# A higher scheduling priority for the chain of states of each head pair in an RWKV-7 layer

## The chip, the cores and the metric

The kernel runs on one core of one Trainium2 chip. The metric is the device time of one execution in microseconds (us). The engines are named as in the profile: PE (TensorE, with PEld for its weight loads), DVE (VectorE), ACT (ScalarE), POOL (GpSimd) and SP (SyncE, which issues most transfers here). Each engine works through its own list of instructions in order; semaphores tie the lists together.

## What is computed

A backbone of two layers over 256 latent tokens of width 1024 with 256 context tokens in front. Layer 0 is a bidirectional RWKV-7 mixer followed by a grouped top-2 mixture of experts, layer 1 a short gated convolution and again experts. The change lies in the mixer's recurrence. Each of 16 heads has a 64x64 state, updated once per token, in both directions; the context is scanned first, and its final state starts the scan over the latent tokens:

```python
def _wkv_scan(decay, k, v, kk, a, r, s0, reverse):
    def step(s, inp):
        w_t, k_t, v_t, kk_t, a_t, r_t = inp
        sa = jnp.einsum('bhvk,bhk->bhv', s, -kk_t)
        s = (s * w_t[:, :, None, :] + sa[..., None] * (kk_t * a_t)[:, :, None, :]
             + v_t[..., None] * k_t[:, :, None, :])
        y = jnp.einsum('bhvk,bhk->bhv', s, r_t) if with_output else None
        return s, y
    return lax.scan(step, s0, xs, reverse=reverse)
...
for p, reverse in enumerate((False, True)):
    s_ctx, yc = _wkv_scan(dec_c, kd_c, v_c, kk_c, a_c, None, s0, reverse)
    _, yl = _wkv_scan(dec_l, kd_l, v_l, kk_l, a_l, r_l, s_ctx, reverse)
    y_lat.append(yl + _bonus(r_l, kd_l, v_l, r_k))
```

The two directions are added, normed per head, multiplied by a gate and projected with w_o. The experts and the second layer follow.

## The kernel before

The recurrence is done in chunks of 64 tokens: 8 chunks (NCH), 4 of context (group g = 0) and 4 of latent tokens (g = 1). Two heads share the 128 partitions, so there are 8 pairs, `fb` = 0 to 7. For each pair the work falls into parts, each written as a Python generator that yields between small pieces:

- **first, second, pre** (together `both`): decays, keys and the operators of all chunks for both directions. The scan `ls` (L704, L706), `kd`, `at`, `bk` (L727 to L744) on DVE; products `pab`, `pat`, `pq` on PE (L766 to L792); `apl`, `at_bd`, `gq`, `hk` copied out of PSUM by ACT (L768, L779, L786, L794); masked into `b_bd`, `gq`, `hk` by DVE (L774, L799, L796).
- **inverse**: the triangular systems of all chunks of the pair at once. ACT packs `apl` into `a_d` (L808, four copies), DVE transposes it (L813), does 31 steps of two operations, a product `lv` (L820) and a subtraction from `t_l` (L822), each reading the result before it, and transposes back into `t_d` (L824). `a_l`, `t_l`, `t_d` exist once, so the inverses of two pairs follow each other.
- **solve**: ACT spreads `t_d` into `d_bd` (L831, four copies for each direction); products (L843) and evictions (`kd`, `bk`, L853 to L862) put the inverse into the operators `rd` and `hk` (L869, L872).
- **chain**: 8 chunk steps for each of two directions, in turn. A step multiplies into a PSUM tile `po` (two buffers): `hk` by the values (L886), plus `rd` by the state `s_bd` of the step before (L893). DVE copies one head's new state out of `po` (L896), ACT the other's (L897), 14 copies each in a pair. In the latent chunks the output goes to `yt`, copied by ACT (L901) for the first direction to reach a chunk and added by DVE (L903) for the second.
- **finish**: bonus, group norm and gate of `yt` (L914 to L938).

What overlaps is written in the loop over pairs. While pair `cur` is solved, half of the next pair's inverse, the finish of the pair before and modulation columns (`adas`) are emitted beside it; while `cur`'s chain runs, the rest of that inverse and the operators of the pair after next (`both(nn)`):

```python
drive((seq(solve(cur, 0), solve(cur, 1)), 20), (half, SPLIT), (finish(prev) if prev else None, 3), ...)
if nxt:
    load_late(nxt)
    drive((chain(cur), 16), (inv, 33 - SPLIT), (both(nn) if nn else None, 22), (adas(ADA2[fb]), ADA2[fb]))
```

`drive` takes turns among its generators in proportion to the weights. That gives the order in which instructions are emitted, and with it their priority. The order on the engines is not this one: a list scheduler goes over the whole program, and of the instructions that its own model holds ready it gives each engine the one of highest priority. So an instruction emitted late can still be placed early when nothing ahead of it is ready. The last pair's chain runs after the loop, under `urgent(..., 200)`, beside the projection `project`.

Of the kernel before, what the change touches and what calls it, by code (L numbers as in the profile page):

```python
# [30 lines left out]
SPLIT = 22  # L31
# [98 lines left out]
class Kern:  # L130
# [63 lines left out]
    def adas(self, n):  # L194
        for _ in range(n):
            if self.todo:
                for _ in self.ada(*self.todo.pop(0)):
                    pass
                yield
# [395 lines left out]
    def rwkv_wkv(self, project_v, right, h, outer):  # L595

        tc, nc, io = self.tc, self.nc, self.io
        with ExitStack() as es:
# [54 lines left out]
            def load(fb):  # L653
                q = Pair()
                q.fb = fb
                q.fs = fs = slice(fb * P, fb * P + P)
                q.kt = two.tile([P, TT], F32, tag="kt", name="kt", bufs=1)
                nc.sync.dma_start(q.kt, self.k_d[fb])
                q.kk = two.tile([P, TT], F32, tag="kkh", name="kkh", bufs=1)
                nc.sync.dma_start(q.kk, self.kk_d[fb])  # L660
                l2 = two.tile([P, 4 * P], F32, tag="l2", name="l2", bufs=1)
                nc.sync.dma_start(l2, io["lora2"][fb][:, :4 * P])
                q.l2 = [two.tile([P, 4 * P], F32R, tag=f"l2{i}", name=f"l2{i}", bufs=1) for i in range(2)]
                nc.scalar.copy(q.l2[0], l2)
                (nc.vector if fb in L2E else nc.gpsimd).tensor_sub(q.l2[1], l2, q.l2[0].bitcast(F32))
                q.rt = two.tile([P, T], F32, tag="rt", name="rt", bufs=1)
                nc.sync.dma_start(q.rt, self.r_d[fb])
                q.ea = [None] * 2
                q.yg = h[:, fb, :]
                q.b = [b_bd[2 * (fb % 2) + d] for d in range(2)]  # L670
                q.at = [at_bd[2 * (fb % 2) + d] for d in range(2)]
                q.rd, q.hk, q.gq = maps[fb % 3]["rd"], maps[fb % 3]["hk"], maps[fb % 2]["gq"]
                return q

            def load_late(q):
                fb, fs = q.fb, q.fs
                q.vt = two2.tile([P, 2, P], F32, tag="vt", name="vt", bufs=2)
                nc.sync.dma_start(q.vt, self.v_d[TC:TT, fs].rearrange("(a p) f -> p a f", p=P))
                q.g2 = two2.tile([P, P], F32, tag="g2", name="g2", bufs=2)
                nc.sync.dma_start(q.g2, io["lora2"][fb][:, 4 * P:])  # L680
                q.vbd = v_bd[fb % 2]
                halves(lambda h, hs: nc.sync.dma_start(
                    q.vbd[hs, :, hs], self.v_d[:, fb * P + 64 * h:fb * P + 64 * h + 64]
                    .rearrange("(c s) f -> s c f", s=64)))
# [117 lines left out]
            def inverse(q):  # L802


                for b in range(4):
                    qs = slice(32 * b, 32 * b + 32)
                    cs = slice(32 * (b % 2), 32 * (b % 2) + 32)
                    nc.scalar.copy(a_d[qs], q.apl.rearrange("p d c t -> p (d c) t")[qs, :, cs])  # L808
                nc.gpsimd.memset(t_l, 0.0)
                for a in range(2):  # L810
                    pcopy(t_l.rearrange("p m r -> p (m r)")[:, a:a + 511:34],
                          self.k("unit", a, a + 1).broadcast_to([P, 16]))
                nc.vector.transpose(out=a_l.rearrange("p j (a u) -> p j a u", a=2),  # L813
                                    in_=a_d.rearrange("p u j -> p j u").unsqueeze(2).broadcast_to([P, 32, 2, 16]))
                yield
                for kk in range(31):
                    m, n = kk // 2 + 1, 31 - kk
                    u = el.tile([P, 144], F32, tag="lv", name="lv")
                    u = u[:, :m * n].rearrange("p (c i) -> p c i", i=n)
                    nc.vector.tensor_mul(u, a_l[:, kk:kk + 1, kk + 1:].broadcast_to([P, m, n]),  # L820
                                         t_l[:, 0:m, kk:kk + 1].broadcast_to([P, m, n]))
                    nc.vector.tensor_sub(t_l[:, 0:m, kk + 1:], t_l[:, 0:m, kk + 1:], u)  # L822
                    yield
                nc.vector.transpose(out=t_d.rearrange("p u j -> p j u"), in_=t_l)  # L824
                yield
# [49 lines left out]
            def chain(q):  # L875
                q.yt = yt = two2.tile([P, 2, P], F32, tag="yt", name="yt", bufs=1)
                po = [[None] * NCH for _ in range(2)]

                def where(i, d):
                    return i // 4, (3 - i % 4 if d else i % 4)  # L880

                def hpart(i, d):
                    g, j = where(i, d)
                    m = 64 if g == 0 else P
                    po[d][i] = pc.tile([P, 512], F32, tag="pc", name="po")[:m, :P]
                    nc.tensor.matmul(po[d][i], q.hk[d][g][:, j], q.vbd[:, 4 * g + j], start=True, stop=i == 0)  # L886
                for i in range(NCH):
                    for d in range(2):
                        g, j = where(i, d)
                        hpart(i, d)  # L890
                        p = po[d][i]
                        if i > 0:
                            nc.tensor.matmul(p, q.rd[d][g][:, j], s_bd[d][i % 2], start=False, stop=True)  # L893
                        if i < NCH - 1:
                            sn = s_bd[d][(i + 1) % 2]
                            nc.vector.tensor_copy(sn[0:64, 0:64], p[0:64, 0:64])  # L896
                            nc.scalar.copy(sn[64:, 64:], p[0:64, 64:])  # L897
                        if g == 1:
                            y = yt[64 * (j % 2):64 * (j % 2) + 64, j // 2, :]
                            if i < 6:  # L900
                                nc.scalar.copy(y, p[64:, :])  # L901
                            else:
                                nc.vector.tensor_add(y, y, p[64:, :])  # L903
                        yield
# [38 lines left out]
            def seq(*gens):  # L943
                for g in gens:
                    yield from g

            def late(n, gen):
                for _ in range(n):
                    yield
                yield from gen  # L950

            def drive(*gw):

                gens = [[g, w, 0.0] for g, w in gw if g is not None]
                while gens:
                    x = min(gens, key=lambda x: x[2])
                    try:
                        next(x[0])
                        x[2] += 1.0 / x[1]
                    except StopIteration:  # L960
                        gens.remove(x)

            def urgent(gen, n):

                done = object()
                while True:
                    with tc.high_priority(n):
                        if next(gen, done) is done:
                            return
                    yield  # L970

            def both(q):
                yield from second(q, 0)
                yield from first(q, 1)
                yield from pre(q, 0)
                yield from second(q, 1)
                yield from pre(q, 1)


            cur = load(0)  # L980
# [24 lines left out]
            for fb in range(NB):  # L1005
                inv = inverse(nxt) if nxt else iter(())
                half = itertools.islice(inv, SPLIT)
                nn = load(fb + 2) if fb + 2 < NB else None
                drive((seq(solve(cur, 0), solve(cur, 1)), 20), (half, SPLIT),
                      (finish(prev) if prev else None, 3), (adas(ADA1[fb]), ADA1[fb]),  # L1010
                      (late(LATE if fb else LATE0, first(nn, 0)) if nn else None, (LATE if fb else LATE0) + 2))
                if nxt:
                    load_late(nxt)
                    drive((chain(cur), 16), (inv, 33 - SPLIT), (both(nn) if nn else None, 22),
                          (adas(ADA2[fb]), ADA2[fb]))
                prev, cur, nxt = cur, nxt, nn

# [898 lines left out]
```

## Time and profile before

| | us |
|---|---|
| median of three runs | 1348.95 (1346.07 to 1351.75) |
| the profiled execution: time | 1347.99 |
| the profiled execution: span of its instructions | 1346.2 |
| the eight pairs, from the first pair's operators to the last chain | about 200 to 640 of the span |
| six periods, from one L813 to the next, pairs 1 to 7 | 258.87 to 571.10, on average 52.0 each |
| busy: PE, DVE, ACT, POOL | 1181.9, 799.9, 606.2, 234.3 |

The profile is of one execution. A window is a stretch of its span; an engine's busy time in it is the sum of its instructions' durations, in which short ones that overlap count twice. "Idle before" is the time an engine stood still ahead of an instruction, with the instruction that released it.

### The profile page before, as it was taken

To read this page: it belongs to the slowest core of one execution; us is meant where nothing else is said; L and a number is where in the kernel's file an instruction comes from. 1 tells how busy PE (TensorE), PEld (TensorE's weight loads), DVE (VectorE), ACT (ScalarE), POOL (GpSimd) and SP (SyncE) were. 2 spreads that over 40 slices of the span, in tenths; PEclk is the share of its full clock that TensorE was granted. 3 is DMA by queue.
4 is the path that set the end of the run, shared out by engine and by line. 5 is a ranking of instruction groups with operands and counts; after the bars stand their busy time and mean duration, and the time that the engine had idled before them with its cause. 6 is when DMAs were issued, how large, how long until landed. Compare 5 with 4: busy or idle time off the path is not lost. (4 is left out here: it accounts for less than half of the span.)

```text
span 1346.2 us, 22273 instructions
## 1 busy us (share of the span) xinstructions
PE 1181.9 (88%) x8608; PEld 851.1 (63%) x8608; DVE 799.9 (59%) x1905; ACT 606.2 (45%) x1219; POOL 234.3 (17%) x245
## 2 busy tenths in 40 slices
PE   3798888789889888899879999889898799999796
PEld 2587688778768777788854444335898744444354
DVE  5869888899998998885442221216667622211145
ACT  4677462656757767645232212215644322212134
POOL 3313442331231231200010000000422300000001
PEclk9799999899999999999989999989899899999898
DMA  9455543233320420226769999999554379999960
GB/s 357 173 172 180 187 143 108 81 122 102 109 93 17 160 77 26 71 102 258 284 237 420 418 420 419 419 413 350 196 177 157 126 299 419 419 420 419 417 262 31
DMA packets 64631, 311.77 MB, mean 232 GB/s; under 512 B 14464, under 2 KB 22912, under 8 KB 29696
## 3 DMA queue, kind: packets, MB, share of 16 engines
q1 hardware_dynamic: 60192, 303.59, 58.4%
q10 hardware_dynamic: 4320, 6.63, 1.3%
q8 instruction: 71, 1.16, 0.3%
q14 instruction: 48, 0.39, 0.1%
HBM read 301.80 MB, written 8.39 MB: 230 GB/s over the span
## 5 line engine op out<-in xcount | busy, mean ns | idle before, releaser
L1565 PE MATMUL wup<-w,xe 128*64 128x512 f32 x960 | 224.7, 611 | 8.7 <-DVEq L1750 8.7
L1565 PEld LDWEIGHTS wup<-w,xe 128*64 128x64 f32 x960 | 65.4, 139 | 121.4 <-issue 114.6
L1581 DVE TENSOR_TENSOR sgate<-sgate,wup 64x512 f32<-64x512 f32 (+1 forms) x32 | 22.1, 689 | 181.8 <-ACT sgate L1580 181.8
L1565 PE MATMUL y<-w,het 128*64 128x512 f32 x480 | 113.9, 599 | 0.0
L1619 DVE SCALAR_TENSOR_TENSOR yy<-y,gw,yy 64x512 fp32r<-64x512 f32 (+1 forms) x64 | 47.8, 750 | 79.8 <-ACT yy L1618 79.3
L1618 ACT ACTIVATE yy<-y,gw 64x512 fp32r<-64x512 f32 (+1 forms) x64 | 43.5, 683 | 111.6 <-PE y L1565 101.0
L1580 ACT ACTIVATE sgate<-wup 64x512 f32<-64x512 f32 (+1 forms) x32 | 18.9, 592 | 158.3 <-PE wup L1565 158.3
L820 DVE TENSOR_TENSOR lv<-a_l,t_l 128x126 f32<-128x126 f32 (+22 forms) x248 | 82.3, 332 | 3.3
L822 DVE TENSOR_TENSOR t_l<-t_l,lv 128x126 f32<-128x126 f32 (+22 forms) x248 | 78.9, 318 | 3.4
L886 PE MATMUL po<-v_bd,hk 128*64 128x128 f32 (+1 forms) x256 | 57.7, 309 | 21.5 <-ACT s_bd L897 7.5
L1565 PEld LDWEIGHTS y<-w,het 128*64 128x64 f32 x480 | 31.5, 136 | 53.2 <-issue 49.1
L1105 ACT CAST wh<-w 128x1024 fp32r<-128x1024 f32 x40 | 41.7, 1046 | 45.0 <-PE dps L143 28.0
L886 PEld LDWEIGHTS po<-v_bd,hk 128*64 128x64 f32 (+1 forms) x256 | 32.3, 165 | 41.8 <-ACT s_bd L897 13.4
L144 PE MATMUL dps<-xh,wl 128*128 128x258 f32 x192 | 55.4, 289 | 3.0 <-POOL wl L1108 3.0
L142 PE MATMUL dps<-xh,wh 128*128 128x258 f32 x192 | 55.3, 288 | 2.8 <-ACT wh L1105 2.8
L1511 PEld LDWEIGHTS xeps<-g,h2t 128*128 128x128 f32 x256 | 36.0, 212 | 32.7 <-issue 27.8
L1797 POOL TENSOR_SCALAR idrw<-cst 128x1024 f32<-128x1024 f32 x2 | 5.5, 2770 | 292.9 <-PE acc L1627 263.9
L722 POOL TENSOR_TENSOR al_bd<-kkh,peb 64x512 f32<-64x512 f32 x32 | 39.8, 1245 | 90.9 <-ACT peb L713 88.2
L143 PE MATMUL dps<-xl,wh 128*128 128x258 f32 x192 | 55.4, 288 | 0.0
L766 PE MATMUL pab<-bk,al_bd 128*128 128x128 f32 x256 | 38.7, 297 | 18.5 <-DVE bk L744 12.7
L1627 PE MATMUL acc<-st,yy 128*128 128x256 f32 x272 | 42.3, 294 | 13.3 <-PEq L1750 9.5
L142 PE MATMUL pps<-x,wh 128*128 128x512 f32 (+1 forms) x128 | 43.6, 361 | 10.4 <-ACT x L361 8.8
(433 smaller groups left out, 3075.9 us busy)
## 6 DMA issues: line engine op xcount, KB each, us to landing
w<-in_wgu SPq DMA_DIRECT2D x128, 1024.0 KB, 13.9
w<-in_wd SPq DMA_DIRECT2D x64, 1024.0 KB, 13.5
w<-in_ada SPq DMA_DIRECT2D x46, 1024.0 KB, 6.5
w<-in_sc_in SPq DMA_DIRECT2D x12, 1024.0 KB, 5.7
w<-in_rk SPq DMA_DIRECT2D x8, 1024.0 KB, 5.4
w<-in_wv SPq DMA_DIRECT2D x4, 1024.0 KB, 5.8
w<-in_wo SPq DMA_DIRECT2D x4, 1024.0 KB, 9.1
w<-in_sc_out SPq DMA_DIRECT2D x4, 1024.0 KB, 5.0
```

Source lines behind the costliest of these rows:

```text
L142: mm(out, lhs[0], rhs[0], start=start, stop=False)
L143: mm(out, lhs[0], rhs[1], start=False, stop=False)
L144: mm(out, lhs[1], rhs[0], start=False, stop=stop)
L722: halves(lambda h, hs: nc.gpsimd.tensor_mul(al_bd[hs, :, 64 * h:64 * h + 64][:, :, ::o], c64(q.kk)[hs], excl[hs]))
L820: nc.vector.tensor_mul(u, a_l[:, kk:kk + 1, kk + 1:].broadcast_to([P, m, n]), t_l[:, 0:m, kk:kk + 1].broadcast_to([P, m, n]))
L822: nc.vector.tensor_sub(t_l[:, 0:m, kk + 1:], t_l[:, 0:m, kk + 1:], u)
L886: nc.tensor.matmul(po[d][i], q.hk[d][g][:, j], q.vbd[:, 4 * g + j], start=True, stop=i == 0)
L1105: self.nc.scalar.copy(h, w)
L1565: nc.tensor.matmul(out[i], a, b[:, 512 * i:512 * i + 512], start=start and q == 0, stop=stop and q == len(sets) - 1)
L1618: nc.scalar.activation(parts[i][0], ys[i], AF.Copy, scale=gws[i])
L1619: nc.vector.scalar_tensor_tensor(parts[i][1], ys[i], gws[i], parts[i][0].bitcast(F32), op0=ALU.mult, op1=ALU.subtract)
L1627: nc.tensor.matmul(acc[4 * i + q], part[:, q * P:q * P + P], st, start=first and q % 2 + k == 0, stop=last and k == len(y) - 1, skip_group ...
```

## The change

In the loop the chain of the current pair is wrapped in `urgent(..., 60)`: each piece of it is emitted inside a block that raises the priority of its instructions by 60, as if they had been emitted 60 instructions earlier. Nothing else differs; the instructions are the same, and the order on the engines is drawn anew. The last pair's chain had such a block before and keeps it.

```diff
--- before.py
+++ after.py
@@ -1011,7 +1011,7 @@
                       (late(LATE if fb else LATE0, first(nn, 0)) if nn else None, (LATE if fb else LATE0) + 2))
                 if nxt:
                     load_late(nxt)
-                    drive((chain(cur), 16), (inv, 33 - SPLIT), (both(nn) if nn else None, 22),
+                    drive((urgent(chain(cur), 60), 16), (inv, 33 - SPLIT), (both(nn) if nn else None, 22),
                           (adas(ADA2[fb]), ADA2[fb]))
                 prev, cur, nxt = cur, nxt, nn
```

`urgent` stands in both kernels:

```python
def urgent(gen, n):
    done = object()
    while True:
        with tc.high_priority(n):
            if next(gen, done) is done:
                return
        yield
```

The first place is DVE at the end of pair 1's inverse (L824) and the start of pair 2's (L813), in the chain of pair 0. Before:

```order
L824 STREAM_TRANSPOSE t_d<-t_l 128x16x32
L896 COPY s_bd_2479<-po 64x64
L896 COPY s_bd_2477<-po 64x64
L774 TENSOR_TENSOR b_bd_1615<-pab,cst 64x4x64 x2
L903 TENSOR_TENSOR yt<-yt,po 64x128
L896 COPY s_bd_2481<-po 64x64
L903 TENSOR_TENSOR yt<-yt,po 64x128
L799 TENSOR_TENSOR gq_1626<-pq,cst 128x512
L796 TENSOR_TENSOR hk_2454<-pq,cst 128x4x64
L903 TENSOR_TENSOR yt<-yt,po 64x128 x2
L919 TENSOR_TENSOR yt<-yt,vt 128x256
L813 STREAM_TRANSPOSE a_l<-a_d 128x1024
```

Now, from the same L824 on:

```order
L824 STREAM_TRANSPOSE t_d<-t_l 128x16x32
L799 TENSOR_TENSOR gq_1626<-pq,cst 128x512
L924 TENSOR_TENSOR vt<-yt 128x256
L796 TENSOR_TENSOR hk_2454<-pq,cst 128x4x64
L925 TENSOR_REDUCE mean<-vt 128x4
L813 STREAM_TRANSPOSE a_l<-a_d 128x1024
L820 TENSOR_TENSOR lv<-a_l,t_l 128x31
L822 TENSOR_TENSOR t_l<-t_l,lv 128x31
L927 RECIPROCAL mean<-mean 128x4
L820 TENSOR_TENSOR lv<-a_l,t_l 128x30
L928 TENSOR_TENSOR yt<-yt,mean 128x256
L822 TENSOR_TENSOR t_l<-t_l,lv 128x30
```

The chain's copies (s_bd), the additions to yt and half of b_bd have left the stretch between L824 and L813, two operations of finish (L924, L925) have entered it, and behind L813 more steps of the inverse (L820, L822) stand directly behind each other.

The second place is ACT at the same point of the program. Before, from the first copy of t_d into d_bd to the last a_d copies:

```order
L831 COPY d_bd<-t_d 32x8x32
L897 COPY s_bd_2479<-po 64x64
L901 COPY yt<-po 64x128
L768 COPY apl<-pab 128x256
L831 COPY d_bd<-t_d 32x8x32
L897 COPY s_bd_2477<-po 64x64
L779 COPY at_bd_1618<-pat 128x512
L831 COPY d_bd<-t_d 32x8x32 x2
L897 COPY s_bd_2481<-po 64x64
L808 COPY a_d<-apl 32x512 x2
L794 COPY hk_2454<-pq 128x4x64
L808 COPY a_d<-apl 32x512 x2
```

Now, from the same pair's last at_bd and hk copies on:

```order
L786 COPY hk_2453<-pq 64x256 x2
L768 COPY apl<-pab 128x256
L779 COPY at_bd_1618<-pat 128x512
L808 COPY a_d<-apl 32x512 x3
L794 COPY hk_2454<-pq 128x4x64
L831 COPY d_bd<-t_d 32x8x32 x4
L808 COPY a_d<-apl 32x512
L926 ACT_TABLE_LOAD
L926 ACTIVATE mean<-mean,eps_gn 128x4
L853 COPY kd<-pq 128x256
L853 COPY bk<-pq 128x512
L696 ACT_TABLE_LOAD
```

The chain's s_bd and yt copies are gone from among the d_bd copies, and three of the four a_d copies stand ahead of them. In the gaps after pairs 2 to 5 all four a_d copies still stand behind d_bd, with hk and one kd eviction (L853) among them; after pair 6 all four stand ahead.

The third place is DVE in the middle of pair 0's chain. Before, from the copy into s_bd_2475 (direction 0) to the next of direction 1:

```order
L896 COPY s_bd_2475<-po 64x64
L820 TENSOR_TENSOR lv<-a_l,t_l 128x121
L704 TENSOR_SCALAR ws<-ws 128x512
L822 TENSOR_TENSOR t_l<-t_l,lv 128x11x11
L706 SCALAR_TENSOR_TENSOR ls<-rst,ws 128x512
L820 TENSOR_TENSOR lv<-a_l,t_l 128x110
L774 TENSOR_TENSOR b_bd_1613<-pab,cst 64x4x64
L822 TENSOR_TENSOR t_l<-t_l,lv 128x11x10
L774 TENSOR_TENSOR b_bd_1613<-pab,cst 64x4x64
L820 TENSOR_TENSOR lv<-a_l,t_l 128x108
L896 COPY s_bd_2479<-po 64x64
```

Now, from that copy on:

```order
L896 COPY s_bd_2475<-po 64x64
L820 TENSOR_TENSOR lv<-a_l,t_l 128x130
L190 STREAM_TRANSPOSE adat<-adaps 128x128
L822 TENSOR_TENSOR t_l<-t_l,lv 128x10x13
L896 COPY s_bd_2479<-po 64x64
L820 TENSOR_TENSOR lv<-a_l,t_l 128x120
L896 COPY s_bd_2477<-po 64x64
L822 TENSOR_TENSOR t_l<-t_l,lv 128x10x12
L191 TENSOR_TENSOR mod_72<-adat,vec 128x8
L742 SCALAR_TENSOR_TENSOR at<-at,kkh 128x512
L820 TENSOR_TENSOR lv<-a_l,t_l 128x121
L896 COPY s_bd_2481<-po 64x64
```

Three copies of the chain follow within eleven rows of the first one where one did.

## Rows read from the trace of the kernel before

**Rows 1.** The page, parts 1 and 2: DVE's busy time and its 40 slices.
```profile
PE 1181.9 (88%) x8608; PEld 851.1 (63%) x8608; DVE 799.9 (59%) x1905; ACT 606.2 (45%) x1219; POOL 234.3 (17%) x245
...
DVE  5869888899998998885442221216667622211145
```

**Rows 2.** Windows: six periods, one period, sum of the six gaps.
```profile
258.87:571.10 312.23, 273.81 (x2483) 236.95 (x2482) 283.91 (x802) 209.93 (x487) 83.79 (x101) 0.99 0.25 83
414.81:467.23 52.42, 46.22 (x445) 40.02 (x445) 48.44 (x139) 35.25 (x83) 13.90 (x17) 1.00 0.32 108
...
sum 41.02, PE 33.75 PEld 30.97 DVE 23.70 ACT 39.18 POOL 6.08; mean PE 5.62 PEld 5.16 DVE 3.95 ACT 6.53 POOL 1.01
```

**Rows 3.** Timeline of DVE at one period's end: start, us, operation, idle before.
```profile
459.89 1.06 DVE L824 STREAM_TRANSPOSE t_d<-t_l 128x512 f32<-128x512 f32 x1
461.20 0.86 DVE L774 TENSOR_TENSOR b_bd<-pab,cst 64x256 f32<-64x256 f32 x2 [0.25 <-ACT apl L768]
...
463.47 0.61 DVE L903 TENSOR_TENSOR yt<-yt,po 64x128 f32<-64x128 f32 x2 [1.03 <-ACT s_bd L897]
464.12 0.69 DVE L799 TENSOR_TENSOR gq<-pq,cst 128x512 f32<-128x512 f32 x1
465.73 0.42 DVE L796 TENSOR_TENSOR hk<-pq,cst 128x256 f32<-128x256 f32 x1 [0.92 <-ACT hk L794]
...
467.23 1.98 DVE L813 STREAM_TRANSPOSE a_l<-a_d 128x1024 f32<-128x1024 f32 x1
```

**Rows 4.** Timeline of ACT over the same end of a period.
```profile
458.77 0.75 ACT L786 COPY gq<-pq 64x256 f32<-64x256 f32 x2
...
461.19 1.41 ACT L831 COPY d_bd<-t_d 32x256 f32<-32x256 f32 x3
462.62 0.59 ACT L779 COPY at_bd<-pat 128x512 f32<-128x512 f32 x1
463.23 0.31 ACT L897 COPY s_bd<-po 64x64 f32<-64x64 f32 x2
...
464.05 1.25 ACT L808 COPY a_d<-apl 32x512 f32<-32x512 f32 x2
465.32 0.37 ACT L794 COPY hk<-pq 128x256 f32<-128x256 f32 x1
...
466.98 0.37 ACT L853 COPY kd<-pq 128x256 f32<-128x256 f32 x1
```

**Rows 5.** Timeline of DVE among the inverse's steps.
```profile
270.41 0.27 DVE L820 TENSOR_TENSOR lv<-a_l,t_l 128x110 f32<-128x110 f32 x1
270.72 0.27 DVE L822 TENSOR_TENSOR t_l<-t_l,lv 128x110 f32<-128x110 f32 x1
271.03 0.29 DVE L820 TENSOR_TENSOR lv<-a_l,t_l 128x126 f32<-128x126 f32 x1
271.24 0.21 DVE L896 COPY s_bd<-po 64x64 f32<-64x64 f32 x1
```

**Rows 6.** Waits of DVE, 258 to 571 us: total, times, longest.
```profile
DVE s_bd L896 <- PE po L893: 2.0, 2, 1.0
```

**Rows 7.** Timeline of DVE in the chains of pairs 6 and 7.
```profile
597.59 0.22 DVE L896 COPY s_bd<-po 64x64 f32<-64x64 f32 x1 [0.35 <-PE po L893]
...
599.58 0.22 DVE L896 COPY s_bd<-po 64x64 f32<-64x64 f32 x1 [0.42 <-PE po L893]
...
627.00 0.22 DVE L896 COPY s_bd<-po 64x64 f32<-64x64 f32 x1 [0.99 <-PE po L893]
```

**Rows 8.** Waits of PE, 258 to 571 us.
```profile
PE po L886 <- ACT s_bd L897: 7.1, 13, 1.2
```

**Rows 9.** Timeline of DVE, finish and the scan behind L813.
```profile
417.08 0.42 DVE L704 TENSOR_SCALAR ws<-ws 128x512 f32<-128x512 f32 x1
...
417.59 1.22 DVE L706 TENSOR_TENSOR_SCAN ls<-rst,ws 128x512 f32<-128x512 f32 x1
...
419.81 0.42 DVE L924 TENSOR_TENSOR vt<-yt 128x256 f32<-128x256 f32 x1
...
420.27 0.41 DVE L925 TENSOR_REDUCE mean<-vt 128x4 f32<-128x256 f32 x1
```

## The prediction

> **What bounds the kernel now.** I read the page first, for the stage: DVE is busy 59% of the span, but 80 to 90% and more in the slices from about 200 to 600 us, which are the pairs [rows 1]. The change touches nothing outside them. Then the windows: I cut the stage at the starts of L813, the transpose that opens each pair's inverse, since that instruction comes once in a pair. Six periods from 258.87 to 571.10 us last 312.2 us, 52.0 us each on average; in the one shown DVE is busy 48.4 of 52.4 us and PE 46.2 [rows 2]. So DVE is the bound and PE stands close behind it.
>
> Next the timeline of DVE. From L813 to L824 (the end of the inverse) it runs nearly without a hole. The holes sit in one place, the gap from the end of one L824 to the next L813 (gap k lies between L824 of pair k and L813 of pair k + 1): there DVE waits 0.25 us for apl, 1.03 us for the chain's copy on ACT, 0.92 us for hk, and L813 itself starts when ACT has delivered a_d [rows 3]. Over six gaps DVE is busy 23.70 of 41.02 us, so it stands still for 17.3 us; ACT is busy 39.18 of the same 41.02 us [rows 2]. The gap is ACT's: four d_bd copies, four a_d copies, at_bd, hk, and between them three or four copies of the chain [rows 4]. 17.3 us is the most that a better order can win here.
>
> **The change part by part.** No instruction is added or removed. The chain's 14 state copies a pair leave the end of the period and stand earlier among the steps of the inverse; finish follows them, and its sums move from behind L813 to before L824.
>
> *The gap.* What ACT still owes between L824 and L813 is read from the new order, priced with the rows of before: d_bd 0.47 each, a_d 0.62, hk 0.37, one solve eviction (kd) 0.37 [rows 4]. What DVE has to do meanwhile: b_bd 0.86, gq 0.69, hk 0.42 [rows 3], and from finish 0.42 and 0.41, in two gaps also the scan of 1.22 with its 0.42 us input step [rows 9].
> - Gap 1: three of four a_d stand ahead of d_bd. ACT owes 4 x 0.47 + 0.62 = 2.5, DVE has 0.69 + 0.42 + 0.42 + 0.41 = 1.9: wait 0.6.
> - Gaps 3 and 5: ACT 1.88 + 0.37 + 2.5 + 0.37 = 5.1; DVE, with the scan, 4.4: wait 0.7 each.
> - Gap 4: ACT 5.1 again, DVE 0.86 + 0.69 + 0.42 + 0.41 + 0.42 = 2.8: wait 2.3.
> - Gap 2: here both b_bd halves and more of finish stand behind L824 (4.8 us of DVE work), but ACT is still at the four gq and hk copies (1.5 us) when L824 ends, and owes at_bd 0.59 besides: about 7.2; wait 2.4.
> - Gap 6: all a_d stand ahead of d_bd: no wait.
>
> Together 6.7 us, and I add the 41.02 - 39.18 = 1.8 us that ACT itself was idle in the gaps, as the hitches between queues that such a count does not see: 8.5 us. Gain 17.3 - 8.5 = 8.8 us. Bounds: nothing (gap 4's 2.3 everywhere would leave 14) to 17.3. I take the middle because the count was made gap by gap, and because the chain's copies (0.31 us for two [rows 4]) really leave ACT's list.
>
> *Exposed steps.* The inverse is a row of 62 operations that each need the one before. Two of them back to back start 0.31 us apart; with another instruction between, the next one starts after 0.21 us [rows 5]. So a step with nothing between costs 0.10 us. In the order, from the first L813 of the loop to the last L824, 119 instructions of DVE stand right behind the one whose result they read; in the changed kernel 152, mostly L820 and L822 behind L813, where finish used to fill the holes. 33 x 0.10 = 3.3 us lost. Bounds 0 to 4.
>
> [...]
>
> *The chain's own waits on DVE.* A copy that stands too soon behind the other waits for PE and holds up all of DVE. Now this happens twice in six periods, 2.0 us in all [rows 6]. The nearest rows for a tighter chain are those of pair 6, whose chain has almost only inverse steps beside it: 13 steps in about 10 us, four waits of which the longest are 0.35 and 0.42 us, 1.1 us in all; with nothing beside it (pair 7) a copy waits up to 1.0 us [rows 7]. In the order of before the second to the last copy of a chain stand over 55 rows of DVE on average (pairs 0 to 5) and over 37 in pair 6; in the changed order over 48. Drawn as a line between 2.0 / 6 = 0.33 us at 55 rows and 1.1 us at 37, that is 0.6 us for each of six chains, 3.6 us, 1.6 more than now. Bounds: 2.0 less, to 6 x 1.1 - 2.0 = 4.8 more.
>
> *Last pairs.* After the sixth period the inverse of pair 7 runs without operator work beside it. Three additions of yt (0.61 for two [rows 3]) move ahead of its L824, a transpose and two small operations behind it; they fill holes either way. I cost it at nothing; uncovered it would be 0.9 us. What follows, the last solve and the experts, is only shifted.
>
> Sum: -8.8 + 3.3 + 1.6 = -3.9 us. On the profiled execution (1347.99 us, span 1346.2) that is 1344.1. It lies 1.0 us below the median of the three runs, 1348.95; against that median the forecast is **1345 us**.
>
> **The rivals.**
> 1. *The gap closes altogether.* If ACT, freed of waiting for the chain, is ahead of my count, only the exposed steps remain: 1348.95 - 17.3 + 3.3 = 1335 us. For it: DVE was late for nearly everything outside the gaps, so ACT and PE have slack there to work ahead. Against it: gaps 2 and 4, where a_d stands behind d_bd and an eviction of the next solve.
> 2. *PE becomes the bound* (slower). PE works in order too. Each chain step begins with a product that needs a po buffer which ACT empties; PE already waits there, 7.1 us behind the state copies [rows 8]. PE has 52.4 - 46.2 = 6.2 us to spare in a period. Close behind each other, 16 steps that wait 0.3 us each use 4.8 of it, and with the other waits of PE it is gone; that is the point from which it decides. At 0.4 us a step PE needs about 54.1 us, 1.7 more in each of six periods: 1348.95 + 10 = 1359 us. For it: pair 7's chain, where the copies go round at PE's pace. Against it: DVE, not PE, was late in the middle of each period.
> 3. *The wait only moves.* ACT's a_d still ends the gap as in gap 4, 2.3 us each time, 14 in all: 3.5 us won, 3.3 lost to exposed steps: 1349 us. The Trainium skill, Perfetto Trace Analysis, section Identifying the Most-Contended Engine and what follows it on strategy, says that a gap which repeats can mean too few buffers; by that the two buffers of po, which the change leaves alone, would keep the gap, with the same result, 1349. The rows name ACT's queue instead.
>
> **How the numbers follow.** Chances: the sum as worked out 0.36, gap closed 0.28, PE bound 0.20, only moved 0.16. Half a per cent, 6.7 us, is about what this measurement can tell from no change (its three runs lie 5.7 us apart). The sum's own range, by its bounds, is 1339 to 1351, and some 0.10 of its 0.36 lies below 1342.2. Faster: 0.28 + 0.10 = 0.38. Same: 0.26 + 0.16 = 0.42. Slower: 0.20. The range takes in rival 1 and most of rival 2: 1334 to 1357 us. The likeliest case alone is 1339 to 1351.
>
> **What would show it.** Right: the gaps from L824 to L813 shrink from 6.8 us to about 4 to 5 on average, DVE's waits for yt on ACT vanish, ACT's d_bd copies run in one row; L820 and L822 behind L813 stand 0.3 us apart. Wrong in the gap: L813 still starts 7 us behind L824, at a_d's pace. Wrong by the chain: rows "s_bd waits for po" on DVE above 6 us, or PE's waits in front of po doubled and DVE's busy share down in the middle of the periods. The prediction fails most easily if periods grow although the gaps shrink.

## The result, and the profile after

The changed kernel takes 1355.0 us in the median of 20 runs, the kernel before 1348.58 us in 20 runs beside it: a ratio of 1.0051 with a 95% interval of 1.004 to 1.0062. The change made the kernel slower. The forecast was 1345 us, with a range of 1334 to 1357: the time lies inside the range, but on the other side of no change.

The page of the changed kernel, parts 1 and 2, answers to [rows 1]: the engines do the same work.

```profile
PE 1188.5 (88%) x8608; PEld 864.2 (64%) x8608; DVE 799.8 (59%) x1905; ACT 605.8 (45%) x1219; POOL 238.3 (18%) x245
...
DVE  5868888898998898874452221115668522221145
```

The stage is cut as before, and two stretches are added: from the last L813 to the end of the last L824 (the inverse of pair 7), and from there to the end of the last L872 (the solve of pair 7). Windows of the kernel before (from and to, the length in us, then the busy time of PE, PEld, DVE, ACT and POOL, PE's granted clock as a share of 2.4 GHz, DMA share, GB/s):

```profile
571.10:601.95 30.85, 29.20 (x314) 25.95 (x314) 27.07 (x102) 12.41 (x35) 0.62 (x1) 1.00 0.23 80
601.95:623.34 21.39, 20.30 (x186) 19.62 (x182) 12.98 (x37) 12.05 (x29) 0.48 (x1) 1.00 0.42 140
```

The same windows of the changed kernel, with the six periods and the sum of the six gaps, which answer to [rows 2]:

```profile
258.30:569.47 311.17, 271.61 (x2466) 241.66 (x2464) 284.89 (x806) 207.09 (x483) 86.86 (x99) 0.97 0.26 84
569.47:605.23 35.76, 33.79 (x288) 30.33 (x288) 27.18 (x99) 14.83 (x40) 0.61 (x3) 0.90 0.07 18
605.23:633.43 28.20, 25.52 (x224) 24.26 (x224) 12.26 (x36) 11.90 (x28) 1.09 (x2) 0.82 0.48 167
...
sum 26.57, PE 18.54 PEld 16.95 DVE 17.35 ACT 25.17 POOL 5.71; mean PE 3.09 PEld 2.82 DVE 2.89 ACT 4.20 POOL 0.95
```

A window's busy time counts overlapping instructions once, not twice as was said ahead of the prediction: DVE's four instructions in gap 1 of the changed kernel add up to 1.94 us, and its window has 1.69 us.

The gaps did shrink, from 41.02 to 26.57 us, and the six periods hardly moved: 312.23 to 311.17 us. The loss lies behind them. The inverse of pair 7 takes 4.9 us more, its solve 6.8 us more; the start is 0.6 us earlier, all that follows 1.2 us longer. Together with the 1.1 us of the periods these are the 11.3 us by which the two spans differ (1346.2 and 1357.5). The profiled execution of the changed kernel was one of its long ones (1359.36 us against the median of 1355.0), so about 5 of the 11.3 us belong to this execution alone; a second profile is below.

The DVE of the changed kernel at the end of a period, beside [rows 3]:

```profile
462.04 1.05 DVE L824 STREAM_TRANSPOSE t_d<-t_l 128x512 f32<-128x512 f32 x1
463.12 0.86 DVE L774 TENSOR_TENSOR b_bd<-pab,cst 64x256 f32<-64x256 f32 x2
464.01 0.69 DVE L799 TENSOR_TENSOR gq<-pq,cst 128x512 f32<-128x512 f32 x1
464.62 0.42 DVE L924 TENSOR_TENSOR vt<-yt 128x256 f32<-128x256 f32 x1
465.07 0.42 DVE L925 TENSOR_REDUCE mean<-vt 128x4 f32<-128x256 f32 x1
465.93 0.42 DVE L796 TENSOR_TENSOR hk<-pq,cst 128x256 f32<-128x256 f32 x1 [0.44 <-ACT hk L794]
468.24 1.97 DVE L813 STREAM_TRANSPOSE a_l<-a_d 128x1024 f32<-128x1024 f32 x1 [1.88 <-ACT a_d L808]
```

And its ACT, beside [rows 4]:

```profile
463.12 1.87 ACT L831 COPY d_bd<-t_d 32x256 f32<-32x256 f32 x4 [0.36 <-DVE t_d L824]
465.02 0.62 ACT L808 COPY a_d<-apl 32x512 f32<-32x512 f32 x1
...
466.96 1.24 ACT L808 COPY a_d<-apl 32x512 f32<-32x512 f32 x2
```

Here is gap 4 as it was forecast: the waits for apl and for the chain's copies are gone, 2.3 us remain, and a_d ends the gap. What was not forecast is PE at such places. The timeline of PE behind pair 6's inverse in the kernel before (one row), and behind pair 6's and pair 7's inverse in the changed kernel:

```profile
568.88 1.95 PE L843 MATMUL pq<-gq,d_bd 128*128 128x64 f32 x16
...
571.36 3.79 PE L843 MATMUL pq<-gq,d_bd 128*128 128x64 f32 x16 [4.22 <-ACT d_bd L831]
574.93 1.81 PE L843 MATMUL pq<-kd,ao_bd 128*128 128x64 f32 x8
...
577.57 1.00 PE L843 MATMUL pq<-kd,d_bd 128*128 128x64 f32 x8
...
607.18 3.59 PE L843 MATMUL pq<-gq,d_bd 128*128 128x64 f32 x16 [2.04 <-ACT d_bd L831]
610.70 1.94 PE L186 MATMUL adaps<-w,sc 128*32 128x128 f32 x32
612.57 1.97 PE L843 MATMUL pq<-kd,ao_bd 128*128 128x64 f32 x8
```

PE stands still for 4.22 and 2.04 us until ACT has copied d_bd. Then the first sixteen products of the solve take 3.79 and 3.59 us where they took 1.95 us before, and the eight behind them 1.81 and 1.97 us where eight of the same shape take 1.00 us a little later. Windows of 4 us show why:

```profile
572.00:576.00 4.00, 4.00 (x21) 4.00 (x20) 3.02 (x14) 1.86 (x4) 0.00 (x0) 0.50 0.01 4
...
608.00:612.00 4.00, 4.00 (x40) 3.68 (x42) 1.06 (x5) 1.26 (x3) 0.00 (x0) 0.50 0.40 170
```

The granted clock is 0.50, the lower of its two levels (1.2 GHz), behind both waits, and PE is busy without a hole in it. Summed from windows of 1 us between 255 and 640 us, PE spends 41 us at the lower level in the changed kernel and 10 us in the kernel before. Before, a hole in front of d_bd was 0.7 us at most.

### The profile page after: what moved, and what is told of

It is laid out like the page before. It is cut to its first block, busy times and chain, and to the rows that moved or that the text cites. A ratio compares the mean times of both kernels' runs of the same rounds, so it can differ in the third digit from the quotient of the medians.

```text
span 1357.5 us, 22291 instructions
## 1 busy us (share of the span) xinstructions
PE 1188.5 (88%) x8608; PEld 864.2 (64%) x8608; DVE 799.8 (59%) x1905; ACT 605.8 (45%) x1219; POOL 238.3 (18%) x245
## 5 line engine op out<-in xcount | busy, mean ns | idle before, releaser
L820 DVE TENSOR_TENSOR lv<-a_l,t_l 128x126 f32<-128x126 f32 (+22 forms) x248 | 80.0, 323 | 4.5
L822 DVE TENSOR_TENSOR t_l<-t_l,lv 128x126 f32<-128x126 f32 (+22 forms) x248 | 78.2, 315 | 4.6
L186 PE MATMUL adaps<-w,sc 128*32 128x128 f32 x1216 | 50.6, 293 | 2.7 <-ACT ws L696 2.3
L142 PE MATMUL pps<-x,wh 128*128 128x512 f32 (+1 forms) x128 | 42.7, 352 | 10.2 <-ACT x L361 8.6
```

Source lines behind the costliest of these rows:

```text
L142: mm(out, lhs[0], rhs[0], start=start, stop=False)
L186: nc.tensor.matmul(ps[32 * j:32 * j + 32, :], self.sc[:, 2 * kc:2 * kc + 32], w[:, P * j:P * j + P], start=kc == 0, stop=kc == NB - 1)
```

## The experiments

All ratios are to the kernel before on the same chip. Every edit lets the scheduler draw the whole order anew, so no run changes one thing alone. Two theories stood at the start. **Theory 1**: the loss sits in the last pair; the periods are about even, because PE, having finished the chain early, waits for d_bd at each period's end, its clock falls, and DVE later waits for PE. **Theory 2**: exposed steps and chain waits of DVE in every period eat the gain and more.

**A second profile.** The changed kernel once more, unedited.

> The changed kernel once more, for a second profile. If the loss after the sixth period is a matter of the order on the engines (PE waits for d_bd behind pair 6's and pair 7's inverse, the modulation columns stand among the products of the last solve), the stretch from the last L813 to the end of the last solve is again 61 to 63 us (first profile 63.2; before 51.5) and PE's clock again falls to half behind both waits. If it was an accident of one execution, the stretch is 52 to 56 us.

Measured: 1356.88 us; six periods 312.20 us, last inverse 36.11, last solve 24.98 us, together 61.1 (the expectation counts this stretch to PE's last product of the solve, 0.7 us less). The loss in the last pair repeats. The solve is 3.2 us shorter than in the first profile, with 3.4 instead of 10.2 us at the lower clock in it: the clock is the part that varies, the order the part that stays.

**Which pairs.** `(urgent(chain(cur), 60) if fb < 6 else chain(cur), 16)`, and the same with `fb == 6`.

> Only the chains of pairs 0 to 5 get the higher priority; pair 6's is as before. Theory 1 (the loss lies in pair 6's chain and what follows, the periods themselves are about even): the last stretch goes back to about 51.5 us and the time to 1346 to 1350 us, ratio 0.998 to 1.001. Theory 2 (exposed steps and waits of DVE in each period eat the gain and more): 1353 to 1355 us, ratio 1.004.

> Only pair 6's chain gets the higher priority. Theory 1: nearly the whole loss, 1353 to 1357 us, ratio 1.003 to 1.006, with waits of PE for d_bd of 2 to 4 us and a halved clock behind them. Theory 2: one seventh of the loss, 1349 to 1350 us.

Measured: pairs 0 to 5 alone 1349.67 us, 1.002 (1.0002 to 1.0039); pair 6 alone 1352.0 us, 1.0038 (1.0023 to 1.0054). One pair of seven makes some three quarters of the loss, where theory 2 had one seventh: theory 2 falls as the account of the whole loss. With pair 6 alone the six periods take 313.1 us and the last stretch 58.5 us (before 52.2). Two details missed: with pairs 0 to 5 the last stretch did not go back (57.3 us, in a profile of its longest execution), because pair 5's chain, which runs beside pair 6's inverse, is early there too, and PE, with nothing left to do, waits 4.1 us for d_bd behind pair 6; and with pair 6 alone PE waited only 0.7 us for d_bd but, late in the last inverse, 2.45 us for the weights of a modulation product, with the clock low from 605 to 613 us. So theory 1 had the place right and named only one of two chains: each of the two runs shows about half of what the last stretch loses, 5.1 and 6.3 us.

**The clock.** Three products without use, ahead of each pair's first solve product, fill PE's wait (PADN is 3; the lines are broken here):

```diff
+warm = lambda pq, n: (pq, [nc.tensor.matmul(pq.rearrange('p j w -> p (j w)'),
+    t_d.rearrange('p u m -> p (u m)')[:, :P], t_d.rearrange('p u m -> p (u m)'),
+    start=True, stop=True) for _ in range(n)])[0]
...
-    pq = pq_.tile([P, 4, P], F32, tag="q", name="pq")[:, :, :w]
+    pq = warm(pq_.tile([P, 4, P], F32, tag="q", name="pq"), PADN if rhs is q.gq[0][0] else 0)[:, :, :w]
```

> The changed kernel with three products of t_d by itself (128x512, results overwritten) ahead of each pair's first product of solve, so that PE works while ACT copies d_bd. Adds 24 products, about 1.8 us each three at full clock, all into time in which PE waited. Theory 1a (the clock that falls in these waits makes the loss): PE's half-clock time between 255 and 640 us falls from 41 us to under 15, and the time to 1346 to 1351 us. Theory 1b (the order in the last pair makes it, whatever the clock): 1354 to 1357 us.

Measured: 1352.49 us, 1.0031 (1.0016 to 1.0046), between the ranges of theories 1a and 1b. The time at the lower clock between 255 and 640 us falls from 41 to 14 us, and the last solve takes 22.9 us, at full clock, where the two profiles above have 28.2 and 25.0:

```profile
606.51:629.42 22.91, 22.12 (x198) 20.18 (x198) 10.54 (x28) 11.84 (x28) 0.48 (x1) 1.00 0.46 151
```

24 products more, and a ratio lower by 0.002 (the two intervals overlap slightly). The last inverse stays at 35.4 us, though PE is at the lower clock for 3.4 us of it in place of 6.8: most of its loss is not the clock's. For the solve the run does not part the clock from the order, since the order changed with the edit: behind pair 6 three of the four a_d copies now stand behind d_bd (that gap is 4.2 us long in place of 0.5), and 26 fewer products fall into the last solve. What shows the clock's part is the pair of profiles of one and the same order above: 3.2 us for 6.8 us more at the lower clock.

**The modulation columns.** `ADA1[7]` from 1 to 0 and `ADA2[7]` from 1 to 2.

> The changed kernel with the modulation columns that were emitted beside pair 7's solve emitted beside its chain instead, so that their 64 products no longer stand among the products of that solve. If they cost what they take there, the last solve (end of the last L824 to the last L872) goes from 25 to 28 us to 22 to 25 us and the time from 1355 to 1352 to 1353 us. If PE's low clock alone makes that solve long, no change: 1354 to 1356 us.

Measured: 1356.35 us, 1.0074 (1.0051 to 1.0098). The last solve falls to 22.7 us as expected (25.0 in the second profile of the changed kernel, with as long at the lower clock), but all that follows, from the start of the chain's last L896 on, takes 715.8 us in place of 710.7. What the columns cost is moved, not saved: the solve went as the first branch had it, the time as the second and a little above it.

**Who is served first at the period's end.** ACT must copy d_bd for PE and a_d for DVE. Priority for the one or the other:

```diff
-    nc.scalar.copy(d_bd[qs, :, qs].rearrange("p c (m a) -> p c m a", a=2),
+    with tc.high_priority(100): nc.scalar.copy(d_bd[qs, :, qs].rearrange("p c (m a) -> p c m a", a=2),
```

```diff
-    nc.scalar.copy(a_d[qs], q.apl.rearrange("p d c t -> p (d c) t")[qs, :, cs])
+    with tc.high_priority(60): nc.scalar.copy(a_d[qs], q.apl.rearrange("p d c t -> p (d c) t")[qs, :, cs])
```

> The changed kernel with priority for ACT's d_bd copies, which PE waits for, over the a_d copies, which DVE waits for. Theory 1 (what hurts is PE standing still for d_bd, the clock behind it, and the late solve of pair 6): gap 6 grows from 0.5 to 0.9 to about 5 us, PE's wait for d_bd of 4.2 us there shrinks to about 2, the last inverse (L813 to the end of L824) falls from 36 to 32 us, time 1349 to 1352 us. Theory 2 (the gap between L824 and L813 is what a period costs): 1357 to 1362 us.

> The opposite: the changed kernel with priority for the a_d copies, so that all four stand ahead of d_bd behind every pair. Theory 2: all gaps close to 0.5 to 1 us as gap 6 did, the six periods lose another 15 to 20 us, time 1336 to 1342 us. Theory 1: the gaps close, but PE waits 4 us for d_bd in every period with half the clock behind it, and DVE gets the time back in waits for PE: six periods 307 to 314 us, time 1349 to 1358 us.

Measured: d_bd first 1358.22 us, 1.0087 (1.0061 to 1.0114); a_d first 1352.2 us, 1.0047 (1.002 to 1.0075). With a_d first DVE's idle time in the gaps is 1.9 us in all, as good as closed, and the periods take 316 us, longer than before. Its windows and waits of DVE (total, times, longest) show where it went:

```profile
254.14:570.12 315.98, 279.86 (x2476) 248.09 (x2474) 287.84 (x808) 207.61 (x485) 88.88 (x101) 0.95 0.26 83
...
DVE ao_bd L835 <- PE pq L843: 6.5, 4, 2.9
DVE s_bd L896 <- PE po L893: 6.0, 13, 1.1
```

DVE gets back as waits for PE inside the inverse what it won in the gap. That was theory 1's branch in the time, though PE's waits for d_bd came to 7.8 us in five places and not to 4 us in each period. It ends the idea of rival 1 that a closed gap is a gain. But d_bd first missed as well: it was to help and has the highest ratio of all. Behind pair 6 it did what was expected (PE waits 1.36 us, the last inverse takes 33.4 us), but its periods are longer (317.8 us), and PE's waits for d_bd in them rise from 7.1 to 11.5 us although d_bd is served first. Neither order of the copies repairs the priority of 60. I read this as too little other work at that place; no run shows it by itself.

**How high.** `urgent(chain(cur), n)` with n of 10, 20 and 40.

> A priority of 20 in place of 60, for all seven chains: the chain ends later in the period, so that PE keeps some of its products for the wait. Theory 1: PE's waits for d_bd at most 1.5 us, low clock between 255 and 640 us under 25 us, time between the two kernels or below, 1346 to 1352 us. Theory 2: the loss grows with the copies that stand early, 1350 to 1353 us.

> A priority of 10 for all seven chains. ACT's s_bd copies still stand among its d_bd copies behind L824, so DVE's wait for yt on ACT stays in the gaps. If what 20 won is that these copies left the gap while DVE kept 5 us of other work for it, 10 wins little: six periods 305 to 312 us, time 1342 to 1348 us. If any earlier chain wins, about half of 20's gain: 1339 to 1342 us.

> A priority of 40 for all seven chains. In the order 8 to 10 rows of DVE stand between L824 and the next L813 (20: 14 to 16, 60: 3 to 13), so too little is left there to cover ACT. If that is what 60 loses against 20, DVE's busy time in a gap falls to 2.5 to 4 us of 4.5 to 5.5, PE waits for d_bd 1 us or more at each end, six periods 303 to 312 us, time 1344 to 1354 us. If 60 loses by something that starts only above 40, time 1334 to 1338 us.

| priority | time, us | ratio (95%) | six periods | last L813 to end of last solve | DVE idle in gaps / between L813 and L824 |
|---|---|---|---|---|---|
| none | 1348.58 | 1 | 312.2 | 52.2 | 17.3 / 11.0 |
| 10 | 1358.59 | 1.0074 (1.0052 to 1.0096) | 321.6 | 56.3 | 15.7 / 20.1 |
| 20 | 1335.7 | 0.9908 (0.9887 to 0.993) | 295.2 | 59.2 | 6.8 / 9.6 |
| 40 | 1350.83 | 1.0021 (1.0008 to 1.0034) | 306.6 | 58.5 | 10.7 / 14.3 |
| 60 | 1355.0 | 1.0051 (1.004 to 1.0062) | 311.2 | 64.0 | 9.2 / 17.1 |

20 is a miss on the good side: no branch had it below 1346 us. (Idle times here and below are the length of a window less DVE's busy time in it, with overlaps counted once.) The DVE of that kernel at the same place of the program, gap 4:

```profile
450.65 1.04 DVE L824 STREAM_TRANSPOSE t_d<-t_l 128x512 f32<-128x512 f32 x1
451.73 0.50 DVE L903 TENSOR_TENSOR yt<-yt,po 64x128 f32<-64x128 f32 x2
...
454.22 0.69 DVE L799 TENSOR_TENSOR gq<-pq,cst 128x512 f32<-128x512 f32 x1 [0.28 <-PE pq L792]
...
457.86 1.98 DVE L813 STREAM_TRANSPOSE a_l<-a_d 128x1024 f32<-128x1024 f32 x1 [0.25 <-ACT a_d L808]
```

And the sum of its six gaps:

```profile
sum 36.53, PE 31.87 PEld 30.60 DVE 29.78 ACT 35.12 POOL 6.08; mean PE 5.31 PEld 5.10 DVE 4.96 ACT 5.85 POOL 1.01
```

The gap is nearly as long as before, since ACT still needs it for d_bd and a_d. But by the windows DVE is busy in 82% of it (before 58% [rows 2], with 60 65%) and PE in 87% (before 82%, with 60 70%): the chain's copies no longer stand in ACT's row, while the last additions to yt, finish and the last operator products still lie there. With 40 and 60 the additions too are done when L824 ends.

10 missed: it was to win a little and loses the most of the four. DVE's waits for yt on ACT grow from 6.3 to 10.2 us, and a new one appears in front of ao_bd; waits of DVE:

```profile
DVE yt L903 <- ACT s_bd L897: 10.2, 11, 1.3
DVE ao_bd L835 <- PE pq L843: 6.4, 2, 4.0
```

That these waits are all that makes 10 lose is not shown.

40 landed in the branch "too little left": DVE is idle for 10.7 of the 29.6 us of its gaps. It wins 5.6 us in the periods, where 20 wins 17.0, and loses 6.2 us in the last stretch. But PE's clock was low for only 10 us between 255 and 640 us, so the low clock is no necessary part of that loss. (Its profile is of one of its shorter executions, span 1343.2 us.)

**20, without pair 6.** `(urgent(chain(cur), 20) if fb < 6 else chain(cur), 16)`

> A priority of 20 for the chains of pairs 0 to 5 alone; pair 6's as before. With 20 for all seven the six periods took 295 us (before 312) but the stretch from the last L813 to the end of the last solve 59 us (before 52). If that loss is pair 6's chain standing ahead of the last inverse on DVE, the stretch goes back to 52 to 55 us, the six periods stay at 294 to 297 us, and the time is 1328 to 1332 us. If the stretch stays at 59 us, pair 6's priority is not what makes it long, and the time is 1335 to 1337 us.

Measured: 1324.6 us, 0.9846 (0.9826 to 0.9866), the fastest of all and below the range of its branch. Windows, with the same three stretches:

```profile
255.39:548.92 293.53, 268.21 (x2489) 235.90 (x2488) 278.98 (x807) 209.80 (x488) 84.05 (x101) 0.99 0.27 89
548.92:578.51 29.59, 28.81 (x315) 25.35 (x318) 25.78 (x96) 12.13 (x34) 0.61 (x1) 1.00 0.23 81
578.51:599.90 21.39, 20.43 (x186) 19.42 (x178) 12.96 (x37) 12.05 (x29) 0.48 (x1) 1.00 0.41 137
```

The last stretch is back at 51.0 us. Waits of DVE in the last inverse with 20 for all seven pairs and, behind the dots, in this kernel tell what pair 6's priority does:

```profile
DVE s_bd L896 <- PE po L893: 4.0, 9, 1.0
...
DVE s_bd L896 <- PE po L893: 1.0, 4, 0.3
```

In the order, pair 6's last chain copy stands 17 rows of DVE ahead of L824 with 20 for all pairs, and 2 rows behind it in this kernel. The chain of pair 6 runs at PE's pace, and a copy of it that stands too early among the inverse's steps makes the last inverse wait (35.4 us with 20 for all, 29.6 here). In earlier pairs the operators of the pair after next stand between; here there are none.

**Why 60 wins nothing in the periods.** Two more kernels, for pairs 0 to 5: the inverse raised together with the chain (`(urgent(inv, 60) if fb < 6 else inv, 33 - SPLIT)` beside it), and the inverse raised alone. Only the part of the inverse that is emitted beside the chain is raised, 11 of its 33 pieces.

> Pairs 0 to 5 only: the chain of the pair and the inverse of the next one both get 60, so that the chain no longer overtakes the inverse and operator work stays for the gap (19 to 25 rows of DVE between L824 and L813 in the order, against 3 to 13 in the changed kernel). If 60 fails in the periods because chain copies push the end of the inverse back until nothing is left to do while ACT packs a_d: gaps of 6 to 9 us with DVE busy over 85% of them, no wait of PE for d_bd above 1 us, six periods 291 to 300 us, time 1324 to 1335 us. If the chain's place among the operators is what costs: six periods 308 to 315 us, time 1344 to 1352 us.

> Pairs 0 to 5 only: the kernel before, with 60 for the next pair's inverse and nothing for the chain. The order keeps ACT's s_bd copies among its d_bd copies, but leaves 15 to 18 rows of DVE in the gap (before 12 to 13). If work left for the gap is all that counts: six periods 294 to 303 us, time 1328 to 1338 us. If the chain's copies must also leave ACT's row there: DVE still waits about 1 us for yt and 1 us for apl in each gap, six periods 305 to 313 us, time 1340 to 1349 us.

Measured: both 1350.4 us, 1.003 (1.0014 to 1.0047); inverse alone 1349.31 us, 1.0016 (1.0001 to 1.0031). With both, the mechanism I expected did not come: gaps of 10 to 14 us, six periods 316.8 us. Waits of PE there:

```profile
PE pab L766 <- DVE bk L744: 16.7, 6, 3.3
```

a_d is packed from apl, and apl comes out of the operators' products pab. Raised so far, the inverse ends before the operators are ready, and the next L813 waits for them, with DVE busy on operators and finish for 52.3 of the 69.6 us of the gaps. With the inverse alone DVE still waits 6.4 us for yt on ACT, as before (6.3): the copies have to leave ACT's row, which was the second branch. So the gap closes from neither side alone. I read the three kernels so that L824 and the operators' last apl have to end together, with the chain's copies out of ACT's row but its last additions still to do, and that 20 hits this point. That it is the only reason is not shown: of the 17.0 us that 20 wins in the periods, 11.9 are idle time of DVE and 5.1 are work that took less time. The rows say where, and not what of the order brought it about: L820 and L822 take 125.0 us there and 130.0 before, L737 2.9 and 5.6, and the longer ones of both stand beside instructions of POOL (last section).

## Why the prediction was wrong

**The gap** was right. Forecast: DVE stands still for 8.5 us of the gaps in place of 17.3. Measured: 9.2 us, and 8.6 in the second profile; waits for yt on ACT are gone, and the last a_d ends each gap. Some luck is in it: gaps 3 and 5 were forecast at 0.7 us each and measured 1.7 and 2.4, gap 2 at 2.4 and measured 1.9, and the 1.8 us added for hitches cover most of the difference. "17.3 us is the most that a better order can win here" was wrong: with 20 for pairs 0 to 5 the six periods are 18.7 us shorter, 10.9 of them idle time in the gaps, 2.9 idle time elsewhere and 4.9 work that took less time.

**Exposed steps** were right. A step right behind its predecessor starts 0.034 us after that one's end, a step behind another instruction on average 0.063 us before its end (77 and 295 steps in the six periods of the kernel before): the 0.10 us of the forecast. In the changed kernel 108 steps stand right behind their predecessor, 31 more: 3.1 us in place of 3.3. The Trainium skill, VectorE: DVE Perf Modes, section The DRAIN you can't avoid, says that the next operation does not start until the pipe is empty, and that one which is not held starts earlier; the 0.063 us agree with the second half.

**The chain's own waits** were right in size and incomplete: s_bd waits for po went from 2.0 to 3.2 us (forecast 3.6; 2.0 in the second profile), but a wait of 2.2 us in front of ao_bd came beside them (last row of the second fence of this section; 1.2 in the second profile). The periods came out at -1.1 us in place of -3.9, and at 0.0 in the second profile: what the gaps won, 8.1 us, went back inside the inverse, where DVE's idle time grew from 11.0 to 17.1 us, and into 1.0 us more of busy time. So in the periods theory 2 has its share.

**The step that failed is the last pairs**: "I cost it at nothing; uncovered it would be 0.9 us. What follows, the last solve and the experts, is only shifted." It measured 11.7 us in one profile and 8.9 in the other. I looked at what moves on DVE there and not at PE and ACT. Behind pair 6's inverse I wrote "no wait", since DVE does not wait; PE does, 4.22 us. The end of that inverse on DVE and the four d_bd copies on ACT:

```profile
567.98 1.03 DVE L824 STREAM_TRANSPOSE t_d<-t_l 128x512 f32<-128x512 f32 x1
...
569.43 1.88 ACT L831 COPY d_bd<-t_d 32x256 f32<-32x256 f32 x4
```

PE has nothing left to do from 567.14 us on, since pair 5's chain is done: 1.9 us pass until L824 ends, 0.4 us while ACT finishes an a_d copy that stands ahead of d_bd, and 1.9 us while it copies d_bd. So the place of a_d is the small part. Before, products of that chain filled the time up to 568.88 us. Pair 6's solve now starts at 571.36 us and at half clock, and the last inverse waits 2.4 us for it in front of ao_bd. Pair 6's own chain does the rest: its copies stand earlier among the steps of the last inverse and wait for PE there, 3.0 us in place of 1.1. The waits of DVE in the last inverse (2.0 us in all before) and, behind the line of dots, two of the six periods:

```profile
DVE ao_bd L835 <- PE pq L843: 2.4, 1, 2.4
DVE s_bd L896 <- PE po L893: 2.2, 6, 0.5
DVE hk L872 <- PE pq L843: 0.9, 2, 0.5
DVE s_bd L896 <- PE po L886: 0.8, 1, 0.8
...
DVE s_bd L896 <- PE po L893: 3.2, 4, 1.1
DVE ao_bd L835 <- PE pq L843: 2.2, 1, 2.2
```

The last solve then begins behind a second hole of PE, with 64 modulation products among its own (14 before).

The sum's own range was too narrow as well: the bounds of its terms, taken together, give about 1330 to 1358 us, and it was set at 1339 to 1351.

**The rivals.** Rival 2 had the right engine and the right sign with the wrong place. Waits of PE in the six periods, before and, behind the dots, in the changed kernel:

```profile
PE po L886 <- DVE yt L903: 2.4, 6, 0.8
PE pq L843 <- ACT d_bd L831: 2.4, 5, 0.7
...
PE po L886 <- DVE yt L903: 8.8, 10, 2.0
PE pq L843 <- ACT d_bd L831: 7.1, 4, 2.2
```

Those for po on ACT's s_bd fell from 7.1 [rows 8] to 1.0 us, but the same product now waits for DVE's additions to yt, so that its waits hardly changed in all (18.7 and 18.2 us in their four largest kinds); those for d_bd rose. Rival 1 is refuted by a_d first, where the gaps closed and the periods grew. Rival 3 had the net of the periods nearly right for a wrong reason: the wait moved, but into the inverse and to PE. The rule beside it, the Trainium skill, Perfetto Trace Analysis, section Optimization Strategy, that a repeating gap can mean too few buffers, does not hold here: with the same two po buffers a priority of 20 took DVE's idle time in the gaps to 6.8 us.

## What to carry to other kernels

A gap in which an engine waits for copies of another is closed either by shorter waiting or by work left to do there. Raising a chain's priority shortens the waiting and takes the work away at once, so its amount has to be tried in steps, and here 20 won 1% where 10, 40 and 60 lost. Ask of every place where one engine is served first which other engine is served last, and what that one still has to do meanwhile. The last round of a software pipeline has no next round to hide behind: cost it apart, on every engine, and leave it out of the change if it does not gain.

## What the runs showed of the hardware that was not expected

PE's clock falls to 0.50 behind waits as short as 1.62 us (486.16 to 487.78 us in the changed kernel), though not behind every one of that length (452.56 to 454.55 us, 1.99 us, has none), and stays there for some 3 to 10 us of work. The Trainium skill, TensorE: Matmul & The Clock Gate, section HAM oscillation — how this bites in real kernels, describes how the clock falls in a wait between bursts of products, so that the next burst starts slow; the wait of 4.22 us behind pair 6 agrees.

Some steps of the inverse take far longer than their neighbours of the same shape. Timelines of DVE and, behind the dots, POOL in the kernel before:

```profile
281.62 1.35 DVE L820 TENSOR_TENSOR lv<-a_l,t_l 128x120 f32<-128x120 f32 x1
...
283.03 0.26 DVE L822 TENSOR_TENSOR t_l<-t_l,lv 128x120 f32<-128x120 f32 x1
...
281.14 1.69 POOL L665 TENSOR_TENSOR l<-l,l 128x512 fp32r<-128x512 f32 x1 [2.19 <-ACT l L664]
```

The long step ends just behind POOL's instruction (282.97 and 282.83 us). In the six periods 51 of the 372 steps take over 0.6 us, all of them beside a POOL instruction; steps with nothing on POOL beside them take 0.25 us on average. What the 51 take above that is some 35 us of the 312, and about 30 in the changed kernel and with 20. The Trainium skill, SBUF — State Buffer, section Who interferes with whom, says that DVE and GpSimd lock each other out of a shared pair of ports; the rows agree. No run took POOL's work away, so what it would give is not shown.
